# A hybrid attention and recurrence block: four whole input tiles added by VectorE, the second value quad ahead of the projection pairs, another last projection block

## The chip, the core and the metric

The kernel runs on one core of a Trainium2 chip. A core has five engines with a queue of instructions each: TensorE (PE, matmuls; its weight loads are listed as PEld), VectorE (DVE), ScalarE (ACT), GpSimd (POOL) and SyncE (SP, which here only issues transfers). Each engine works its own queue strictly in order; a wait on a semaphore holds everything behind it on that engine. The metric is device microseconds of one execution; less is better.

## The reference

```python
def hybrid_layer(x, layer, norm1_g, w_in, b_gate, lb_logits, hg_norm_g, w_o_sb, w_o_hg, w_out,
                 norm2_g, w_ff1, w_ff2):
    xn = rmsnorm(x, norm1_g[layer])
    u = xn @ w_in[layer].astype(f32)
    q_sb, k_sb, v_sb, f_raw, i_hg, q_hg, g_hg, gate_sb, gate_hg = jnp.split(u, list(c), axis=-1)
    o_sb = stick_breaking_attention(...)       # 8 heads of 64, causal, log space, blocks of 128 queries
    ...
    f = lb + (1.0 - lb) * sig                  # sig = sigmoid(f_raw)
    k_hg = (1.0 - lb) * jax.nn.sigmoid(-f_raw)
    o_hg = hgrn2_chunkwise(silu(q_hg), k_hg, i_hg, log(f))    # 4 heads of 128, chunks of 64
    o_hg = rmsnorm(o_hg, ...)
    o_hg = merge_heads(o_hg) * jax.nn.silu(g_hg)
    ...
```

1024 tokens of 1024 channels go through an RMSNorm; one wide projection gives queries, keys and values of 8 attention heads, the four inputs f, i, q, g of a 4-head gated recurrence (HGRN2), and two gates. Stick-breaking attention and the recurrence run on the same normalised input; their outputs are merged by sigmoid gates, projected, added to x, and followed by a squared-ReLU MLP of width 4096 and a last RMSNorm. All is float32.

## The kernel before

A float32 matrix is split into a high and a low part of a rounded format, hi = round(x) (a cast by ACT) and lo = x - hi (a subtraction by DVE), and a product is three matmuls: hi·hi, hi·lo and lo·hi. Names ending in h and l are such parts (xnh/xnl the normalised input, wv1h/wv1l the weights of the second value quad), names with r are raw weights as loaded.

The stages on PE are, in order:

- the front: transposes of x, the normalised input in eight tiles (half 0 and half 1 of the tokens, four each), the query/key projection of attention head 0 (`pjqk`), the value projection of heads 0 to 3 (`pjv` with wv0, 8 token blocks) and that of heads 4 to 7 (wv1, 8 token blocks, the job `j_v`). One token block is two steps of the stream `front`, 24 matmuls of 256 columns;
- four projection pairs (`ProjPair`): two blocks of 128 output columns are formed together from seven products m1 to m7 instead of eight, each of 12 matmuls of 512 columns (`ppX`, `ppY`, `ppZ`). This needs sums of input tiles: `early_whole` adds hi and lo back to whole tiles `xw`, `early_sums` adds whole tiles together and splits the sums into efh/efl. The eight blocks are the queries and keys of heads 1 to 7 and one further block, f of recurrence head 0;
- the attention loop over 64 items (8 heads, 8 query blocks): scores `z` from the tiles KS, QH, QL, a scan `rm` on DVE, a turn `pw` on PE, weights wTh/wTl, values `po`. KS, QH, QL of a head are written to DRAM by the projection and loaded again by SP (`qk_load`). Between items PE works off filler steps from the stream `st`: raw gate products (`raw_job`: `pga`, `pgq`, 36 matmuls of 512 columns), the i projection (`i_job`: `pji`), f, q and g projections (`hg_job`). `n_fill` filler jobs' steps are spread over the 64 items;
- the recurrence, head by head, with the rest of the stream as filler (`sl`, `pk` are its own products; `upto` bounds the filler for each head), then the merge, and the MLP.

What sets the order: each engine's queue is fixed when the program is built, from the order in which the code records operations and from buffer ownership. SP issues all loads one after another in the order of the code, and a load whose buffer is still in use holds those behind it. Raw weights have two buffers. POOL issues the stores of v, q and k, and in `early_whole(0)` it adds the four whole tiles of half 0.

Of the kernel before, what the change touches and what calls it, by code (L numbers as in the profile page):

```python
# [13 lines left out]
AF = mybir.ActivationFunctionType  # L14
ALU = mybir.AluOpType
# [24 lines left out]
def kernel(  # L40
# [67 lines left out]
    def after(ins, earlier):  # L108
        if earlier is not None and earlier.ins is not ins.ins:
            tc.add_manual_dep(ins.ins, earlier.ins.name, NOSYNC, reason="issue order")  # L110
        return ins
# [643 lines left out]
    def first_job():  # L755
        name, u_qk, ep = qk_item(0)
        u_qk.__class__ = FirstUnit
        u_v = v_unit(0)

        def body():  # L760
            v_ep = v_epilogue(0)
            for half, parts in enumerate((((0, 2), (2, 2)), ((0, 4),))):
                ps = bank(f"{name}_{half}")
                for b0, n in parts:
                    ts = slice(b0 * P, (b0 + n) * P)
                    yield from proj_half(ps[:, ts], u_qk.hl[0], xn.mov, KT, half, ts=ts)
                    if b0 + n == 4:
                        ep(ps, half)
                    if half == 0 and b0 > 0:
                        front.prefetch()  # L770
                    tb = 4 * half + b0
                    yield from token_steps("pjv0", u_v, xn, range(tb, tb + n), v_ep, tb == 0)

        return front.add([u_qk], body), u_qk, u_v
# [6 lines left out]
    def early_whole(half_, engine):  # L781
        for kp in range(KT // 2):
            h, l = (t.bitcast(F32) for t in xn.t[half_, kp])
            early[half_, kp // 2, kp % 2] = t = slot(f"xw{half_}{kp}")
            after(engine.tensor_tensor(out=t, in0=h, in1=l, op=ALU.add), last_power[0])

    early_forms = {}

# [130 lines left out]

    def qk_parts(h):  # L920
        return ((C_Q + h * DHS, DHS), (C_K + h * DHS, DHS)), qk_store(h)

    QB_ORDER = (7, 0, 6, 1, 5, 2, 4, 3)
    items = [(h, qb) for h in range(NHS) for qb in QB_ORDER]
# [167 lines left out]
    def i_job(h):  # L1092
        unit = wide_unit(f"wi{h}", W_IN, C_I + h * P)
        pair = {}

        def ep(ps, tb):
            i, c = tb // 2, tb % 2 * 256
            if c == 0:
                pair[i] = half(f"i{h}_{i}")
            nc.scalar.copy(pair[i][:, c : c + 256], ps)  # L1100
            if c:
                rows_ = irows[i * 256 : (i + 1) * 256, h * P : (h + 2) * P]
                nc.gpsimd.dma_start(
                    rows_.rearrange("(t p) c -> p t c", p=P),
                    pair.pop(i).rearrange("p (t c) -> p t c", t=2),
                )

        unit.late = h == 0

        def body():  # L1110
            for i, _ in enumerate(token_steps(f"pji{h}", unit, xn, range(NT), ep)):
                yield
                if unit.late and i == 6:
                    hi_behind[0] = turn_hi[0]
                    st.prefetch()
                    hi_behind[0] = None

        return st.add([unit], body)

    def i_load(h):  # L1120
        hg[h, "v"] = slot(f"v{h}")
# [467 lines left out]


    j_raw = [raw_job(0)]
    hg_job(0, "q")
    i_job(0)
    i_job(2)
    hg_job(0, "g")
    j_first_hg = j_hg[0]
    for h in range(1, NHG):
        hg_jobs(h)
        if h < NHG - 1:
            j_raw.append(raw_job(h))  # L1600
    j_raw += [raw_job(cb) for cb in range(len(j_raw), KT)]
    j_sb = [sb_job(cp) for cp in range(4)]

# [731 lines left out]
    lower_bounds()  # L2335
    front.advance(11, j_first)
    first_row()
    early_whole(0, nc.gpsimd)
    early_whole(1, nc.vector)
    early_sums()  # L2340
    blocks = [qk_parts(h) for h in range(1, NHS)] + [(((C_F, P),), f_epilogue(0))]
    proj = [ProjPair(i, *blocks[2 * i : 2 * i + 2]) for i in range(4)]
    front.finish(j_first)
    front.advance(8, j_v)
    proj[0].load()
    proj[0].split_plain()
    proj[0].m1()
# [1 line left out]
    for o, n in zip(proj, proj[1:] + [None]):  # L2349
        o.m2()  # L2350
        if n:
            n.load()
        o.m6()
        if not n:
            qk_load(0)
            v_load(0)
        o.m5()
        if n:
            n.split_plain()
        o.m7()  # L2360
        if n:
            n.m1()
            n.split_sums()
        o.m4()
        if not n:
            scores(*items[0])
            weights(*items[0])
        o.m3()
    v_split(0)
    front.advance(4, j_v)  # L2370
    scores(*items[1])
    front.advance(5, j_v)

    n_fill = 7 + 2 * 9 + 2 * 17
    n_first = 0
    ready = deque()
    wsums = out_weight_sums()
# [1 line left out]
    for i, it in enumerate(items):  # L2379
# [5 lines left out]
            next(wsums, None)  # L2385
        ahead = it[0] + 1
        if ahead < NHS and i % NHS in (2, 3, 5):
            if ahead == NHS // 2:
                front.finish(j_v)
            {2: qk_load, 3: v_load, 5: v_split}[i % NHS](ahead)  # L2390
        want = n_first + (i + 1) * (n_fill - n_first) // len(items)
        for _ in range(want - done):
            if front.pos < j_v:
                front.step()
            else:
                st.advance(1, j_first_hg)
        done = want
        before = ready.popleft() if ready else None

# [19 lines left out]
    for h in range(NHG + 1):  # L2419
# [2 lines left out]
        upto = (j_hg[2], j_hg[3], j_raw[6], j_sb[1], j_sb[3])[h]  # L2422
        if h > 0:
            i_load(h - 1)
        going = True
        while going:
            going = False
# [112 lines left out]
```

## Time and profile before

| | |
|---|---|
| median of 3 runs | 1492.26 us (1490.87 to 1496.12) |
| the profiled execution's own time | 1493.49 us |
| its span | 1491.8 us |
| PE busy | 1440.0 us, 97% of the span |
| DVE busy | 1106.6 us, 74% |
| ACT busy | 656.4 us, 44% |
| POOL busy | 177.2 us, 12% |
| mean granted PE clock | 0.985 |

The profiled execution lies 1.2 us above the median, and its span 1.7 us below its own time. A row of a timeline reads: start in us, duration in us, engine, line, operation, output<-inputs, shape, number of instructions run together, and in brackets how long the engine had been idle and what released it. A row of the table of waits reads: engine, line that waited, what it waited for, us in total, times, longest. A window row reads: stretch, length, busy us of PE, PEld, DVE, ACT and POOL with counts, granted PE clock, DMA share, GB/s.

### The profile page before, as it was taken

How to read it: one execution, taken by the hardware profiler on the slowest of the kernel's cores; microseconds unless marked ns; L12 is line 12 of the kernel's file. 1: busy time of each engine (PE TensorE's matmuls, PEld its weight loads, DVE VectorE, ACT ScalarE, POOL GpSimd, SP SyncE). 2: the span in 40 equal slices, each digit the busy share in tenths (PEclk: the TensorE clock that was granted, in tenths of full speed). 3: DMA queues.
4: the chain of work that ended last, by engine and by line, in shares of the span. 5: the costliest groups of instructions: out<-in, count | busy, mean ns of one | idle time of the engine just before them, and what ended most of it. 6: DMA issues, size and time to landing. Idle time of an engine off the chain costs nothing. (4 is left out here: it accounts for less than half of the span.)

```text
span 1491.8 us, 19878 instructions
## 1 busy us (share of the span) xinstructions
PE 1440.0 (97%) x7422; PEld 1223.7 (82%) x7422; DVE 1106.6 (74%) x1538; ACT 656.4 (44%) x1064; POOL 177.2 (12%) x322
## 2 busy tenths in 40 slices
PE   8899989899999999899998999999999999999997
PEld 8787879898888888788887888888888888888886
DVE  6964588788976789968775889766766656768755
ACT  6344456466232334343334485544444443433433
POOL 5212222232001012110011120000000000000031
PEclk9899999999999999999999999999999999999999
DMA  7146656765222258554559543444444985666824
GB/s 233 51 142 187 180 155 150 146 121 129 63 67 67 75 161 216 175 175 156 169 157 282 196 170 112 147 147 148 148 152 149 341 311 209 225 251 245 287 101 188
DMA packets 165945, 253.00 MB, mean 170 GB/s; under 512 B 27052, under 2 KB 95192, under 8 KB 165848
## 3 DMA queue, kind: packets, MB, share of 16 engines
q1 hardware_dynamic: 146392, 195.87, 40.1%
q0 software_dynamic: 15712, 49.30, 12.2%
q10 hardware_dynamic: 3744, 6.56, 1.2%
q8 instruction: 58, 0.95, 0.3%
q14 instruction: 39, 0.32, 0.1%
HBM read 181.43 MB, written 74.45 MB: 172 GB/s over the span
## 5 line engine op out<-in xcount | busy, mean ns | idle before, releaser
L972 DVE TENSOR_TENSOR_SCAN rm<-rm,bits 128x512 f32<-128x512 f32 (+6 forms) x72 | 87.6, 1223 | 20.2 <-ACT rm L946 19.8
L154 ACT CAST whid<-w 128x1024 fp32r<-128x1024 f32 x30 | 31.6, 1053 | 154.3 <-PE pm L131 90.1
L131 PE MATMUL pm<-wlod,sh 128*128 128x512 f32 x240 | 93.5, 389 | 0.1
L131 PE MATMUL pm<-whid,sl 128*128 128x512 f32 x240 | 93.4, 389 | 0.0
L131 PE MATMUL pm<-whid,sh 128*128 128x512 f32 x240 | 93.4, 389 | 0.0
L131 PE MATMUL pm<-tl,sh 128*128 128x512 f32 (+1 forms) x210 | 81.3, 387 | 0.0
L131 PE MATMUL pm<-th,sl 128*128 128x512 f32 (+1 forms) x210 | 81.3, 387 | 0.0
L131 PE MATMUL pm<-th,sh 128*128 128x512 f32 (+1 forms) x210 | 81.3, 387 | 0.0
L159 DVE TENSOR_TENSOR wlod<-w,whid 128x1024 fp32r<-128x1024 f32 x30 | 36.7, 1222 | 56.9 <-ACT whid L154 56.9
L2148 POOL TENSOR_SCALAR fss<-fss 128x1 f32<-128x1 f32 x8 | 4.0, 494 | 562.1 <-ACT fsc L2143 561.6
L159 DVE TENSOR_TENSOR sl<-sa,sh 128x1024 fp32r<-128x1024 f32 x56 | 68.2, 1218 | 0.5 <-ACT sh L154 0.5
L1020 ACT ACTIVATE wTh<-pw,minus_one 128x512 fp32r<-128x512 f32 (+2 forms) x96 | 53.4, 585 | 24.7 <-PE pw L134 23.9
L154 ACT CAST sh<-sa 128x1024 fp32r<-128x1024 f32 x56 | 57.2, 1046 | 6.7 <-DMA sa<-ad 6.7
L1026 DVE SCALAR_TENSOR_TENSOR wTl<-pw,wTh 128x512 fp32r<-128x512 f32 (+2 forms) x96 | 49.9, 545 | 7.5 <-ACT wTh L1020 6.9
L131 PEld LDWEIGHTS pm<-wlod,sh 128*128 128x128 f32 x240 | 45.0, 187 | 9.9 <-DVE wlod L159 0.6
L131 PEld LDWEIGHTS pm<-whid,sl 128*128 128x128 f32 x240 | 45.1, 188 | 9.4
L131 PEld LDWEIGHTS pm<-whid,sh 128*128 128x128 f32 x240 | 45.1, 188 | 9.3
L131 PE MATMUL pX<-sql,t1h 128*128 128x512 f32 x128 | 50.0, 391 | 0.1
L131 PE MATMUL pX<-sqh,t1l 128*128 128x512 f32 x128 | 49.8, 389 | 0.0
L131 PE MATMUL pX<-sqh,t1h 128*128 128x512 f32 x128 | 49.8, 389 | 0.0
L131 PE MATMUL po<-wTh,V 128*128 128x256 f32 x160 | 43.5, 303 | 3.7 <-ACT wTh L1020 3.7
L946 ACT ACTIVATE rm<-z 128x512 f32<-128x512 f32 (+3 forms) x96 | 44.0, 492 | 6.4 <-PE z L131 4.2
(965 smaller groups left out, 4610.0 us busy)
## 6 DMA issues: line engine op xcount, KB each, us to landing
w<-in_w_ff_dram SPq DMA_DIRECT2D x72, 512.0 KB, 5.1
sa<-ad SPq DMA_DIRECT2D x56, 512.0 KB, 6.4
ad<-a SPq DMA_DIRECT2D x32, 256.0 KB, 4.2
ad<-s SPq DMA_DIRECT2D x16, 512.0 KB, 5.7
tw<-in_w_out_dram POOLq DMA_DIRECT2D x24, 256.0 KB, 6.8
x<-in_x_dram SPq DMA_DIRECT2D x8, 512.0 KB, 8.6
qkh<-qkh POOLq DMA_DIRECT2D x16, 256.0 KB, 3.0
qkl<-qkl POOLq DMA_DIRECT2D x16, 256.0 KB, 3.2
```

Source lines behind the costliest of these rows:

```text
L131: return pe(nc.tensor.matmul(*a, **k))
L154: hi_last[0] = after(in_turn("act", nc.scalar.copy(dst, src)), hi_behind[0])
L159: nc.vector.tensor_tensor(out=dst, in0=src, in1=hi.bitcast(F32), op=ALU.subtract),
L946: nc.scalar.activation(rm[:, s0 : s0 + m], z[:, :m], AF.Sigmoid, scale=-0.125)
L972: sc = nc.vector.tensor_tensor_scan(out=rr, data0=rr, data1=bits[:, 1024 - nk + a : 1024 - nk + b][:, ::-1], initial=rm[:, b : b + 1] if i ...
L1020: nc.scalar.activation(th[:, 0:n, qs], src, AF.Identity, bias=minus_one),
L1026: nc.vector.scalar_tensor_tensor(out=tl[:, 0:n, qs], in0=src, scalar=-1.0, in1=th[:, 0:n, qs].bitcast(F32), op0=ALU.add, op1=ALU.subtract,),
L2148: nc.gpsimd.tensor_scalar(out=ssq, in0=ssq, scalar1=1.0 / D, scalar2=EPS, op0=ALU.mult, op1=ALU.add)
```

## The change

Six edits, all of order and place; the number of matmuls is the same.

1. The whole tiles of half 0 are added by VectorE instead of GpSimd, after those of half 1.
2. The loads and splits of the second value quad's weights (two casts, two subtractions) are recorded after the first job's second half instead of in the middle of it.
3. All 8 token blocks of the second value quad run before the pairs; before it was 4, and 4 behind the pairs.
4. The last block of the last pair is the g of recurrence head 0 instead of its f: its silu is stored to DRAM and loaded again by POOL when recurrence head 1 begins. The f of head 0 becomes a filler job.
5. `qk_load(0)` and `v_load(0)` come before m7 of the third pair instead of after m6 of the fourth, and the scores of the first two items between the fourth pair's products.
6. The filler stream is raw0, i0, raw1, i2, f0, q0, then heads 1 to 3 with raw2 between (before: raw0, q0, i0, i2, g0, then heads with raw1 to raw3 between). One raw job more lies in the attention loop (`n_fill` 59 to 66), and the loop no longer runs steps of the value quad. The special prefetch in `i_job` is gone.

```diff
--- before.py
+++ after.py
@@ -766,8 +766,6 @@
                     yield from proj_half(ps[:, ts], u_qk.hl[0], xn.mov, KT, half, ts=ts)
                     if b0 + n == 4:
                         ep(ps, half)
-                    if half == 0 and b0 > 0:
-                        front.prefetch()
                     tb = 4 * half + b0
                     yield from token_steps("pjv0", u_v, xn, range(tb, tb + n), v_ep, tb == 0)
 
@@ -782,7 +780,7 @@
         for kp in range(KT // 2):
             h, l = (t.bitcast(F32) for t in xn.t[half_, kp])
             early[half_, kp // 2, kp % 2] = t = slot(f"xw{half_}{kp}")
-            after(engine.tensor_tensor(out=t, in0=h, in1=l, op=ALU.add), last_power[0])
+            engine.tensor_tensor(out=t, in0=h, in1=l, op=ALU.add)
 
     early_forms = {}
 
@@ -919,6 +917,15 @@
 
     def qk_parts(h):
         return ((C_Q + h * DHS, DHS), (C_K + h * DHS, DHS)), qk_store(h)
+
+    gsd = dram("gs0", [P, T])
+
+    def g_store(src, half_):
+        cs = slice(half_ * 512, (half_ + 1) * 512)
+        t = half(f"g0_{half_}")
+        nc.scalar.activation(t, src, AF.Sigmoid)
+        mul(t, src, t)
+        nc.gpsimd.dma_start(gsd[:, cs], t)
 
     QB_ORDER = (7, 0, 6, 1, 5, 2, 4, 3)
     items = [(h, qb) for h in range(NHS) for qb in QB_ORDER]
@@ -1105,17 +1112,7 @@
                     pair.pop(i).rearrange("p (t c) -> p t c", t=2),
                 )
 
-        unit.late = h == 0
-
-        def body():
-            for i, _ in enumerate(token_steps(f"pji{h}", unit, xn, range(NT), ep)):
-                yield
-                if unit.late and i == 6:
-                    hi_behind[0] = turn_hi[0]
-                    st.prefetch()
-                    hi_behind[0] = None
-
-        return st.add([unit], body)
+        return st.add([unit], lambda: token_steps(f"pji{h}", unit, xn, range(NT), ep))
 
     def i_load(h):
         hg[h, "v"] = slot(f"v{h}")
@@ -1589,15 +1586,16 @@
 
 
     j_raw = [raw_job(0)]
+    i_job(0)
+    j_raw.append(raw_job(1))
+    i_job(2)
+    hg_job(0, "f")
     hg_job(0, "q")
-    i_job(0)
-    i_job(2)
-    hg_job(0, "g")
     j_first_hg = j_hg[0]
-    for h in range(1, NHG):
+    hg_jobs(1)
+    j_raw.append(raw_job(2))
+    for h in range(2, NHG):
         hg_jobs(h)
-        if h < NHG - 1:
-            j_raw.append(raw_job(h))
     j_raw += [raw_job(cb) for cb in range(len(j_raw), KT)]
     j_sb = [sb_job(cp) for cp in range(4)]
 
@@ -2335,13 +2333,14 @@
     lower_bounds()
     front.advance(11, j_first)
     first_row()
-    early_whole(0, nc.gpsimd)
+    front.prefetch()
     early_whole(1, nc.vector)
+    early_whole(0, nc.vector)
     early_sums()
-    blocks = [qk_parts(h) for h in range(1, NHS)] + [(((C_F, P),), f_epilogue(0))]
+    blocks = [qk_parts(h) for h in range(1, NHS)] + [(((C_GH, P),), g_store)]
     proj = [ProjPair(i, *blocks[2 * i : 2 * i + 2]) for i in range(4)]
     front.finish(j_first)
-    front.advance(8, j_v)
+    front.finish(j_v)
     proj[0].load()
     proj[0].split_plain()
     proj[0].m1()
@@ -2350,28 +2349,28 @@
         o.m2()
         if n:
             n.load()
+        else:
+            scores(*items[0])
         o.m6()
         if not n:
-            qk_load(0)
-            v_load(0)
+            weights(*items[0])
         o.m5()
         if n:
             n.split_plain()
+        else:
+            scores(*items[1])
+        if o is proj[-2]:
+            qk_load(0)
+            v_load(0)
         o.m7()
         if n:
             n.m1()
             n.split_sums()
         o.m4()
-        if not n:
-            scores(*items[0])
-            weights(*items[0])
         o.m3()
     v_split(0)
-    front.advance(4, j_v)
-    scores(*items[1])
-    front.advance(5, j_v)
-
-    n_fill = 7 + 2 * 9 + 2 * 17
+
+    n_fill = 2 * 7 + 2 * 9 + 2 * 17
     n_first = 0
     ready = deque()
     wsums = out_weight_sums()
@@ -2385,15 +2384,10 @@
             next(wsums, None)
         ahead = it[0] + 1
         if ahead < NHS and i % NHS in (2, 3, 5):
-            if ahead == NHS // 2:
-                front.finish(j_v)
             {2: qk_load, 3: v_load, 5: v_split}[i % NHS](ahead)
         want = n_first + (i + 1) * (n_fill - n_first) // len(items)
         for _ in range(want - done):
-            if front.pos < j_v:
-                front.step()
-            else:
-                st.advance(1, j_first_hg)
+            st.advance(1, j_first_hg)
         done = want
         before = ready.popleft() if ready else None
 
@@ -2422,6 +2416,9 @@
         upto = (j_hg[2], j_hg[3], j_raw[6], j_sb[1], j_sb[3])[h]
         if h > 0:
             i_load(h - 1)
+        if h == 1:
+            hg[0, "g"] = slot("g0")
+            nc.gpsimd.dma_start(hg[0, "g"], gsd)
         going = True
         while going:
             going = False
```

On DVE, near the end of the front (qkl is the low part of head 0's queries and keys, xnt a transpose of x in PSUM). Before:

```order
L159 TENSOR_TENSOR qkl_0_476<-pjqk_0_282,qkh_0_475 128x512
L159 TENSOR_TENSOR wv1l_486<-wv1r_481,wv1h_485 128x1024
L159 TENSOR_TENSOR wv1l_490<-wv1r_483,wv1h_489 128x1024
L335 SCALAR_TENSOR_TENSOR xnl_548<-xnt_0_549,prm,xnh_547 128x512
L335 SCALAR_TENSOR_TENSOR xnl_548<-xnt_0_556,prm,xnh_547 128x512
L335 SCALAR_TENSOR_TENSOR xnl_564<-xnt_0_565,prm,xnh_563 128x512
```

Now (the eight xnl of the second half follow the first qkl directly; this piece stands behind them):

```order
L159 TENSOR_TENSOR qkl_1_637<-pjqk_1_611,qkh_1_636 128x512
L159 TENSOR_TENSOR wv1l_744<-wv1r_739,wv1h_743 128x1024
L159 TENSOR_TENSOR wv1l_748<-wv1r_741,wv1h_747 128x1024
L783 TENSOR_TENSOR xw_751<-xnh_536,xnl_537 128x1024
L783 TENSOR_TENSOR xw_753<-xnh_552,xnl_553 128x1024
L783 TENSOR_TENSOR xw_755<-xnh_568,xnl_569 128x1024
L783 TENSOR_TENSOR xw_757<-xnh_584,xnl_585 128x1024
L783 TENSOR_TENSOR xw_759<-xnh_247,xnl_248 128x1024
```

The two wv1l subtractions moved from ahead of the eight xnl to behind the second qkl, and DVE has eight whole-tile additions there, four of them POOL's before.

On SP, the loads at the start of the attention loop (KS and QH of the next head, wi0r/wi2r the raw i weights, wga1r the raw gate weights, wq0r those of q). Before:

```order
L139 DMA QL_1732<-qkl_102 64x1024 x2
L139 DMA wq0r_1776<-in_w_in_dram 128x8x128
L139 DMA wi0r_1782<-in_w_in_dram 128x4x256
L139 DMA wi0r_1784<-in_w_in_dram 128x4x256
L139 DMA wi2r_1967<-in_w_in_dram 128x4x256
L139 DMA wi2r_1969<-in_w_in_dram 128x4x256
L139 DMA KS_2041<-qkh_103 64x1024
```

Now:

```order
L139 DMA QL_1737<-qkl_102 64x1024 x2
L139 DMA wi0r_1750<-in_w_in_dram 128x4x256
L139 DMA wi0r_1752<-in_w_in_dram 128x4x256
L139 DMA wga1r_1762<-in_w_in_dram 128x8x128
L139 DMA wga1r_1764<-in_w_in_dram 128x8x128
L139 DMA wi2r_1940<-in_w_in_dram 128x4x256
L139 DMA wi2r_1942<-in_w_in_dram 128x4x256
L139 DMA KS_2074<-qkh_103 64x1024
```

The load of wq0r is gone from here and the two of wga1r stand between those of wi0r and wi2r.

On PE, the end of the recurrence's levels of head 3 (sl the level products, pk the state's, pot and pys filler). Before:

```order
L131 MATMUL pys_1_6122<-asbh_5660,wo01l_5900 128x512
L131 MATMUL sl_5_6133<-q_5176,k_5065 32x32 x16
L131 MATMUL pys_1_6122<-asbh_5757,wo01h_5899 128x512
L131 MATMUL pys_1_6122<-asbl_5758,wo01h_5899 128x512
L131 MATMUL pys_1_6122<-asbh_5757,wo01l_5900 128x512
L131 MATMUL pys_1_6122<-asbh_5869,wo01h_5899 128x512
L131 MATMUL pys_1_6122<-asbl_5870,wo01h_5899 128x512
L131 MATMUL pys_1_6122<-asbh_5869,wo01l_5900 128x512
L131 MATMUL sl_6_6169<-q_5176,k_5065 64x64 x8
L134 MATMUL pk_0_6193<-ident,k_5065 128x128 x4
```

Now:

```order
L131 MATMUL pys_1_6104<-asbh_5824,wo01l_5845 128x512
L131 MATMUL sl_4_0_6126<-q_5138,k_5024 128x128 x4
L131 MATMUL sl_4_1_6131<-q_5138,k_5024 128x128 x4
L134 MATMUL pot_1_6144<-ident,hon_1_6007 128x128 x4
L131 MATMUL sl_5_6150<-q_5138,k_5024 32x32 x16
L131 MATMUL sl_6_6175<-q_5138,k_5024 64x64 x8
L134 MATMUL pk_0_6199<-ident,k_5024 128x128 x4
```

Between sl_4 and pk there stood 36 filler matmuls of 512 columns (the last 12 around sl_5 are seen above); now there is none beside the transposes pot. From the end of head 2's pk to head 3's, the filler has 126 such matmuls, where it had 162.

## The prediction

> **What bounds the kernel now.** I read the page first, then PE's table of waits, then the windows, and only then single rows around each wait.
>
> ```profile
> PE 1440.0 (97%) x7422; PEld 1223.7 (82%) x7422; DVE 1106.6 (74%) x1538; ACT 656.4 (44%) x1064; POOL 177.2 (12%) x322
> PE ppar L215 <- DVE xnl L335: 9.0, 1, 9.0
> PE z L131 <- DMA QH<-qkh: 8.0, 2, 4.4
> PE pwW L131 <- DVE h L1395: 4.2, 1, 4.2
> PE sl L131 <- DVE pp L167: 4.0, 1, 4.0
> PE po L131 <- ACT wTh L1020: 3.7, 3, 1.9
> PE pw L134 <- ACT i L1100: 3.5, 1, 3.5
> PE pgq L131 <- ACT wga0t L154: 2.5, 1, 2.5
> PE pk L134 <- DVE k L167: 1.4, 1, 1.4
> ```
>
> PE is busy 97% and the change leaves its matmuls alone, so what can move is PE's idle time, some 50 us, and the slow clock behind each wait. The change touches all but pwW of these. The windows say where they lie, and that the clock falls with them (column behind POOL):
>
> ```profile
> 40.00:60.00 20.00, 15.91 (x93) 14.28 (x94) 19.48 (x27) 1.84 (x5) 4.29 (x5) 0.79 0.20 57
> 60.00:80.00 20.00, 20.00 (x149) 19.12 (x149) 18.99 (x20) 13.03 (x18) 2.72 (x4) 1.00 0.15 50
> 140.00:160.00 20.00, 16.39 (x75) 13.45 (x74) 6.76 (x10) 6.85 (x11) 3.47 (x5) 0.91 0.91 226
> 160.00:180.00 20.00, 17.49 (x122) 16.07 (x122) 12.25 (x16) 8.87 (x20) 6.61 (x16) 0.96 0.71 192
> 200.00:220.00 20.00, 15.60 (x85) 13.28 (x84) 14.60 (x22) 8.80 (x19) 4.66 (x13) 0.91 0.85 211
> 260.00:280.00 20.00, 15.06 (x98) 14.20 (x98) 13.85 (x18) 9.39 (x21) 4.55 (x12) 0.84 0.48 90
> 600.00:650.00 50.00, 44.59 (x262) 37.57 (x261) 45.27 (x76) 21.55 (x42) 7.18 (x11) 0.93 0.54 172
> ```
>
> **The front (edits 1 to 3).** The 9.0 us are the largest term. The timeline of DVE, POOL and PE shows their cause:
>
> ```profile
> 14.23 2.36 DVE L159 TENSOR_TENSOR wv0l<-wv0r,wv0h 128x1024 fp32r<-128x1024 f32 x2
> 30.98 12.05 DVE L159 TENSOR_TENSOR wv1l<-wv1r,wv1h 128x1024 fp32r<-128x1024 f32 x2
> 32.70 9.25 POOL L785 TENSOR_TENSOR xw<-xnh,xnl 128x1024 f32<-128x1024 f32 x4
> 42.96 3.37 DVE L335 SCALAR_TENSOR_TENSOR xnl<-xnt,prm,xnh 128x512 fp32r<-128x512 f32 x5
> 43.75 0.32 PE L215 MATMUL ppar<-ident,prow 36*128 36x36 f32 x1 [9.01 <-DVE xnl L335]
> 50.99 0.39 PE L131 MATMUL pjqk<-xnh,wqk0wlo 128*128 128x512 f32 x1
> 51.67 0.39 PE L131 MATMUL pjqk<-xnh,wqk0wlo 128*128 128x512 f32 x1
> 51.90 0.28 PE L131 MATMUL pjv<-wv0h,xnh 128*128 128x256 f32 x1
> ```
>
> Two subtractions that take 2.36 us for wv0 took 12.05 for wv1, and the 9.7 us more are POOL's 9.25 of additions: the two engines did not work side by side. DVE's xnl stood behind, and PE behind them. In the changed order the eight xnl follow the first qkl at once, and POOL adds nothing. With 3.37/5 = 0.67 us each from about 32.4 on, they end at 37.7, a pair each 1.35 us; PE comes to ppar at 43.75 − 9.01 = 34.74 and uses a pair per 6 matmuls at 0.227 us (51.67 − 50.99 over three), 1.36 us, so it finds each there. `pjqk` then ends at 34.74 + 0.3 + 24×0.227 = 40.5 where it ended at 51.9: **−11.4 us**, 9.0 of the wait and the rest slow clock (0.79 in that window).
>
> This time must not be lost again ahead of the pairs, since DVE was full there (19.48 and 18.99 of 20). It gets 4 more whole tiles and the wv1 subtractions:
>
> ```profile
> L785 POOL TENSOR_TENSOR xw<-xnh,xnl x4: 2329/2335/2372, 32.7 to 39.6; 128x1024 f32<-128x1024 f32 x4
> L785 DVE TENSOR_TENSOR xw<-xnh,xnl x4: 1214/1216/1220, 49.7 to 54.6; 128x1024 f32<-128x1024 f32 x4
> 54.97 0.37 ACT L663 COPY v<-pjv 128x256 f32<-128x256 f32 x1 [2.29 <-PE pjv L131]
> 57.85 0.37 ACT L663 COPY v<-pjv 128x256 f32<-128x256 f32 x1 [2.51 <-PE pjv L131]
> 77.79 1.22 DVE L159 TENSOR_TENSOR wlob<-wp0b,whib 128x1024 fp32r<-128x1024 f32 x1 [0.39 <-ACT whib L154]
> 80.40 0.39 PE L131 MATMUL ppX<-efh,whib 128*128 128x512 f32 x1
> ```
>
> A token block of the value quad takes PE 57.85 − 54.97 = 2.88 us; 4 of them now run ahead of the pairs, 11.5 us, so m1 begins when it did (40.5 + 4×2.88 + 8×2.88 = 75.1, and m6 at 80.5 against 80.40), with 11.5 us of later work done. DVE is free at 42, does wv1 to 44.4 (first needed by the second quad at 52.0), then eight whole tiles. The first sum of whole tiles starts at 44.4 + 8×1.14 = 53.5, where it started at 55.7 (54.6 + 1.14); the rest of the chain is the same, so wlob is ready by 77, some 3 us ahead of m6. Hence nothing for the moved additions; their cover is that second quad. Without it they would cost 4×1.14 + 2.36 = 6.9 less these 3.
>
> **The end of the pairs (edits 4, 5).** PE's first wait for QH:
>
> ```profile
> 138.84 0.45 SPq L139 DMA_DIRECT2D QH<-qkh  x1
> 149.45 0.73 PE L131 MATMUL z<-KS,QH 128*128 128x512 f32 x2 [3.61 <-DMA QH<-qkh]
> 150.97 0.63 PE L131 MATMUL ppX<-xnl,w54h 128*128 128x512 f32 x1
> 151.40 0.63 PE L131 MATMUL ppX<-xnh,w54l 128*128 128x512 f32 x1
> 202.48 0.65 SPq L139 DMA_DIRECT2D QH<-qkh  x1
> 216.36 1.19 PE L131 MATMUL z<-KS,QH 128*128 128x512 f32 x2 [4.40 <-DMA QH<-qkh]
> QH<-qkh SPq DMA_DIRECT2D x2, 256.0 KB, 12.4
> wi2r<-in_w_in_dram SPq DMA_DIRECT2D x2, 512.0 KB, 5.4
> ```
>
> QH was issued at 138.84, when the fourth pair's m6 let go of its buffer, and its data came 10.6 us later. Its issue now stands a pair earlier on SP, and the buffers it takes are let go by the first two pairs: that is 20 us and more ahead of z. The 3.61 us go, and with them 9 matmuls at 0.427 in place of 0.227 us (151.40 − 150.97; they are 0.63 long where 0.39 is usual): 3.61 + 1.8 = **−5.4 us**. g's silu store is two halves of ACT, DVE and POOL work in place of f's; none of these engines is full in 140 to 160 (6.76, 6.85 and 3.47 of 20), so nothing.
>
> On the slow clock the Trainium skill ("TensorE: Matmul & The Clock Gate", "What's actually happening") says that PE falls to half rate after an idle window of about 3.4 us. The rows agree for the waits of 3.6 and 4.4, but the wait of 2.5 for pgq is also followed by a clock of 0.96. By the rule each long wait adds up to 1.7 us; the sum would differ by under 1.
>
> **The start of the attention loop (edit 6).** The second wait for QH, 4.40 at 216.36, has its load issued at 202.48, behind wi2r on SP, with 12.4 us to landing since the DMA engines were at 0.85. PE had 216.36 − 4.40 − 202.48 = 9.5 us of work in that time. Now SP comes to it when wga1's splits let a buffer go, and by the filler that stands from there to the second head's z PE has 14 to 15. The price with the slow rows behind is 4.4 + 1.4 = 5.8; I take **−4.5** (0 to −5.8).
>
> The third, 3.5 for pw, and 1.42 behind it for po:
>
> ```profile
> 270.79 1.04 ACT L154 CAST wg0h<-wg0r 128x1024 fp32r<-128x1024 f32 x1 [6.78 <-DMA wg0r<-in_w_in_dram]
> ```
>
> ACT stood 6.78 us at this cast while its copy of i and its wTh were queued behind. wg0 leaves the loop; wf0 takes its place behind wi2's buffer, its cast some 6 us after its issue, nearly the landing time (5.4 for wi2r). Of 3.5 + 1.4 + 1.4 = 6.3 I take **−4** (0 to −6.3).
>
> New there are the loads of wi0 and wga1 close ahead of their casts, each behind a buffer that the one before must let go. ACT or DVE can stand at these as ACT stood for wg0: **+1.5** (0, as behind the pair's weights, to 4, two thirds of that case). q0 now is the last filler before the recurrence needs q: **+0.5** (0 to 1.5, below pk's 1.4). The wait for wga0t, 2.5, has the same cast ahead of it as before; I leave it.
>
> **The recurrence (edit 6).** The raw job that went into the attention loop is missing here. In head 3's stretch PE waited 4.0 + 1.4 = 5.4 us for DVE, which was at 45.27 of 50. Between the second head's pk and the third's the filler falls from 162 to 126 matmuls, 36×0.227 = 8.2 us of PE; DVE loses the job's splits:
>
> ```profile
> 400.97 1.22 DVE L1395 TENSOR_TENSOR wga1r<-wga1r,wga1r 128x1024 f32<-128x1024 f32 x1
> ```
>
> Two of this size and three of half of it (two more for the weights, and the sum of p1 and p4), at 1.22 and some 0.69, are 4.5 us. Where DVE sets the pace, PE gains no time from less filler beyond these 4.5: idle grows by 8.2 − 4.5 = 3.7. I take **+4** (1.5, with 2.4 us of DVE's waits for loads gone, to 7, with DVE's part not shortened in the stretch that counts). In the attention loop the same 8.2 us fill nothing that the trace shows as idle; it counts once, as PE work.
>
> **Sum.** −11.4 −5.4 −4.5 −4 +1.5 +0.5 +4 = −19.3, from the profiled execution's 1493.5: **1474 us**, or 1473 as the median stands 1.2 lower. With all ends good it is −28 (1465), with all bad −11.4 −5.4 +4 +1.5 +7 = −4.3 (1489).
>
> **The rivals.**
>
> A: *the attention loop only trades its waits.* SP's order there is new, every raw weight has just two buffers, and a wait removed in a chain of loads may stand a load further on. Then the second and third wait bring nothing, and with +1.5, +0.5 and the recurrence's full 7 it is 1493.5 − 16.8 + 9 = **1486**. For it: three waits in 176 to 273 had three different loads as cause. Against: PE has more filler per item.
>
> B, on the other side: *casts at the head of ACT's queue.* wi0, wga1, wi2, wf0 come in a row, each cast waiting 6.78 as wg0h did, PE losing 6.3 each. Without the gain on the second and third wait, and with the recurrence's 4 and q0's 0.5, −12.3 is there to be eaten; from two such waits it is even, and from three (+18.9) it is slower: **1500**. Against: the row of wg0h is the only cast in the loop that stood so long.
>
> C: *the change doesn't do what it says in the front.* If the 12.05 us are not POOL's doing (the trace shows only that they coincide) but a late input of the second subtraction, the wait goes with wv1 to another place, behind the second qkl, and stops the second quad: −11.4 becomes −1.7, which gives **1484**.
>
> D: *DVE becomes the bound ahead of the pairs.* Should its chain slip by the 6.9 us added, wlob is there at 79.0 + 6.9 = 85.9, for m6's third matmul at 80.9: +5.0, **1479**. The Trainium skill speaks for it ("Perfetto Trace Analysis", "Optimizing Scalar/DVE Operations"): a saturated DVE is to hand work to others; it adds that a hand-over to GpSimd may not help, as they share a port. POOL's 2.33 us for DVE's 1.22, and DVE standing for all of them, agree with the second half.
>
> **How the numbers follow.** Forecast 0.58, A 0.20, B 0.07, C 0.08, D 0.07. The range 1463 to 1489 holds the forecast's own ends, A, C and D at their times, and leaves out B and the bad ends of A. A measurement of this kernel tells 0.3%, 4.5 us, from no change: below 1487.8 is faster. Of the forecast's 0.58 nearly all is, of A 0.13, of C 0.06, of D all: 0.83; no change 0.10; slower 0.07 from B.
>
> **What would show it.** In the changed profile PE should have no wait over 1 us at ppar, POOL no xw row, DVE's wv1l 2.4 us; the window 40 to 60 PE full at clock 1.00; m6 at about 80 and the fourth pair ahead of the loop ending near where it did; no wait for QH at the first z and one under 2 us at the second head's; PE's waits for DVE in the recurrence 8 to 11 us in place of 5.4. A wait of several us at m1, m6 or pjv's second quad proves C or D; rows of casts idle over 5 us for wi or wga loads prove B. The forecast is wrong if PE's idle time in 40 to 300 does not fall by some 15 us, or if the recurrence's grows by over 8.

## The result, and the profile after

| | before | changed |
|---|---|---|
| median | 1492.64 us (1490.87 to 1496.12, 4 runs) | 1474.63 us (1470.48 to 1475.80, 4 runs) |
| profiled execution | 1493.49 us, span 1491.8 | 1475.80 us, span 1474.1 |
| mean granted PE clock | 0.985 | 0.988 |

The ratio is 0.9872, 95% interval 0.9845 to 0.9898: 1.3% faster, where 1474 was forecast.

From PE's table of waits in the changed kernel (engine, line, what it waited for, us in total, times, longest):

```profile
PE sl L131 <- DVE pp L167: 5.7, 2, 4.2
PE pwW L131 <- DVE h L1392: 5.5, 1, 5.5
PE po L131 <- DVE wTl L1033: 4.2, 4, 2.3
PE pji L131 <- DVE wTl L1033: 2.4, 1, 2.4
PE po L131 <- ACT wTh L1027: 2.0, 3, 1.1
PE pjqk L131 <- DVE xnl L335: 1.8, 1, 1.8
PE pgq L131 <- ACT wga0t L154: 1.4, 1, 1.4
PE pgq L131 <- DVE wga0t L159: 1.1, 1, 1.1
PE pw L134 <- ACT rm L953: 1.1, 1, 1.1
```

The 9.0 at ppar and both waits for QH are gone; the 1.8 at pjqk lie in the first half of the front, at 11.92, ahead of what the edits move. What remains from the fourth pair to the end of the attention loop is short, and spread over po, pji, pgq and pw. Three waits are longer than before: the one for pp in the recurrence (5.7, where it was 4.0 and 1.4 more at pk), the one for h in the merge, and po's for wTl (4.2, 2.7 before). Windows of 20 us of the changed kernel (columns as before):

```profile
40.00:60.00 20.00, 20.00 (x160) 19.61 (x160) 17.81 (x21) 5.03 (x10) 3.62 (x6) 1.00 0.43 106
140.00:160.00 20.00, 19.83 (x95) 16.20 (x93) 14.55 (x20) 11.02 (x20) 6.83 (x17) 1.00 0.87 256
160.00:180.00 20.00, 17.50 (x100) 15.21 (x101) 13.93 (x18) 12.32 (x23) 4.62 (x12) 0.91 0.70 215
180.00:200.00 20.00, 17.74 (x131) 17.17 (x130) 17.28 (x25) 10.24 (x24) 4.48 (x10) 0.91 0.66 173
260.00:280.00 20.00, 15.66 (x122) 14.72 (x122) 15.95 (x21) 10.77 (x25) 4.88 (x8) 1.00 0.78 185
```

40 to 60 is full at clock 1.00 (15.91 and 0.79 before) and 140 to 160 nearly so. The stretches 160 to 200 and 260 to 280 still have 2 to 4 us of idle PE each, the first two with a lowered clock.

To place the gain, I took for each kernel the start of certain matmuls minus the streaming time of all matmuls ahead of them in PE's order (0.2265 us per 512 columns, at least 0.05 for one). The difference is the time lost up to there, with a constant part that is equal in all kernels, so that only the differences down a column mean something; the table has its growth by stage, in us. "To pair 1" ends at m1's first matmul, "pairs" at the last `ppX`, "to po" at the first values, "loop" at the last values, "recurrence" at head 3's pk, "rest" at the last matmul of the MLP.

| kernel | to pair 1 | pairs | to po | loop | recurrence | rest | all |
|---|---|---|---|---|---|---|---|
| before | 26.9 | 5.4 | 6.0 | 43.7 | 43.3 | 19.3 | 144.6 |
| changed | 17.7 | 0.3 | 5.7 | 38.4 | 43.9 | 21.0 | 127.0 |
| changed, profiled again | 15.9 | 0.3 | 5.7 | 41.3 | 43.7 | 19.4 | 126.3 |
| GpSimd adds beside xnl | 15.7 | 1.1 | 4.0 | 41.6 | 43.8 | 19.5 | 125.7 |
| before, edit 1 only | 17.5 | 8.8 | 7.6 | 44.6 | 44.1 | 18.3 | 140.9 |
| before, edits 1 and 2 | 15.4 | 12.6 | 7.1 | 46.0 | 43.7 | 20.6 | 145.4 |
| before, edits 1 to 3 | 16.3 | 0.2 | 12.6 | 45.5 | 43.0 | 20.0 | 137.6 |
| changed without edit 5 | 16.0 | 0.2 | 9.0 | 38.6 | 43.8 | 18.2 | 125.8 |
| second raw job back | 16.0 | 0.4 | 4.9 | 31.9 | 43.7 | 19.5 | 116.4 |
| old stream order | 16.0 | 0.4 | 4.6 | 33.6 | 45.0 | 19.5 | 119.1 |
| old order, old prefetch | 16.4 | 0.3 | 4.0 | 32.9 | 44.0 | 20.2 | 117.8 |

So the changed kernel won 9 to 11 us before the pairs, 5 in the pairs, 2 to 5 in the loop, and lost nothing in the recurrence. One execution differs from another by 1 to 3 us in a stage: in its first profile the changed kernel came to the first `pjv` at 16.13 us, in its second at 14.38, and the kernel before at 14.66.

### The profile page after: what moved, and what is told of

It reads as the page before. It is cut to its first block, busy times and chain, and to the rows that moved or that the text cites. A ratio compares the mean times of both kernels' runs of the same rounds, so it can differ in the third digit from the quotient of the medians.

```text
span 1474.1 us, 19891 instructions
## 1 busy us (share of the span) xinstructions
PE 1437.2 (97%) x7422; PEld 1222.6 (83%) x7422; DVE 1102.5 (75%) x1542; ACT 656.5 (45%) x1064; POOL 173.8 (12%) x321
## 5 line engine op out<-in xcount | busy, mean ns | idle before, releaser
L131 PE MATMUL po<-wTl,V 128*128 128x256 f32 x160 | 42.1, 296 | 4.3 <-DVE wTl L1033 4.2
L131 PEld LDWEIGHTS pm<-tl,sh 128*128 128x128 f32 x210 | 39.4, 188 | 8.2
```

The source lines that it names most:

```text
L131: return pe(nc.tensor.matmul(*a, **k))
```

## The experiments

All are timed against the kernel before on the same chip; where no interval is named, medians are meant. The kernel before spread more on these chips (1477.8 to 1495.6) than on the first, so the intervals of the ratios are some 0.3 to 0.7% to each side, and small differences are read from the stages above. Three chips were used: one for the first four experiments, one for "Edit 5 undone", the second raw job, the old order and the filler in head 3's levels, one for the rest. Where kernels of different chips are set side by side, that is a comparison of medians alone.

**What held up the second half's input.** GpSimd adds the four whole tiles again, beside the xnl; the rest is the changed kernel.

```diff
-            engine.tensor_tensor(out=t, in0=h, in1=l, op=ALU.add)
+            r = engine.tensor_tensor(out=t, in0=h, in1=l, op=ALU.add)
+            if half_ == 0:
+                after(r, last_power[0])
...
+    early_whole(0, nc.gpsimd)
     front.advance(11, j_first)
...
     early_whole(1, nc.vector)
-    early_whole(0, nc.vector)
```

> The changed kernel, with the four whole tiles of half 0 added by GpSimd again, recorded ahead of the first job's second half so that they run beside the eight xnl. If GpSimd's additions hold up whatever DVE does (the prediction's reading), the eight xnl, 5.4 us in the changed kernel, last about 14 to 15, PE waits some 8 to 9 us ahead of or in pjqk, and the time rises by 7 to 11 us, less up to 4.6 us for four additions fewer on DVE if these are on its path. If they hold up only an operation that takes both inputs from SBUF (xnl takes one from PSUM), xnl keeps 5.4 us and the time is the changed kernel's within 2 us. If GpSimd was not the cause, wv1l takes 2.4 us here too and nothing else moves.

1474.4 us, beside 1474.6 and 1474.0 for the changed kernel: no difference. The timeline of DVE and POOL in this kernel:

```profile
32.10 5.36 DVE L335 SCALAR_TENSOR_TENSOR xnl<-xnt,prm,xnh 128x512 fp32r<-128x512 f32 x8 [1.41 <-ACT xnh L332]
32.35 9.45 POOL L783 TENSOR_TENSOR xw<-xnh,xnl 128x1024 f32<-128x1024 f32 x4
37.60 4.23 DVE L226 TENSOR_TENSOR lmx<-prm 128x4 f32<-128x4 f32 x1
41.86 0.24 DVE L230 TENSOR_TENSOR le<-prm,lmx 128x4 f32<-128x4 f32 x2
```

The eight xnl, whose xnt lies in PSUM, take 5.36 us with GpSimd adding beside them, exactly as without. The operation behind them, on 4 columns and with both its inputs in SBUF, takes 4.23 us, until GpSimd's last addition ends at 41.80; operations of that size take some 0.2 elsewhere. The copy of prm just before it, out of PSUM, takes 0.18. So GpSimd did hold DVE up, but only operations with both inputs in SBUF: in the kernel before, the wv1 subtractions. Moving these two behind the xnl (edit 2) is enough; who adds the whole tiles (edit 1) makes no difference to the time of the changed kernel. The Trainium skill ("SBUF — State Buffer", "SBUF: two separate sides") says the same, that GpSimd and a DVE operation with two SBUF inputs lock each other out for the length of an instruction. Here the wait was longer than that: GpSimd's instructions end about every 2.36 us (9.45/4), and the small operation waited from 37.60 past an end at about 39.4 to the last one.

**Edit 1 alone**, in the kernel before.

```diff
-            after(engine.tensor_tensor(out=t, in0=h, in1=l, op=ALU.add), last_power[0])
+            engine.tensor_tensor(out=t, in0=h, in1=l, op=ALU.add)
...
-    early_whole(0, nc.gpsimd)
     early_whole(1, nc.vector)
+    early_whole(0, nc.vector)
```

> The kernel before, with only the four whole tiles of half 0 moved to DVE; the two wv1 subtractions stay ahead of the xnl, half of the second quad stays behind the pairs. If GpSimd held up DVE: wv1l takes 2.4 us in place of 12, PE's wait at ppar falls from 9.0 to under 1.5 us, and PE then stands ahead of m6 instead, since DVE's chain to wlob ends only some 3 us sooner: the time falls by 2 to 5 us. Rival, a late input of the second subtraction: wv1l stays at about 12 us and the time at 1492, within 2.

1491.05 us, ratio 1.0006 (0.9971 to 1.0041). Its timeline:

```profile
30.91 2.35 DVE L159 TENSOR_TENSOR wv1l<-wv1r,wv1h 128x1024 fp32r<-128x1024 f32 x2
75.52 0.79 PE L131 MATMUL ppX<-efh,whib 128*128 128x512 f32 x1 [3.36 <-ACT whib L154]
```

wv1l is 2.35 us, so the late-input rival falls. Of the 9.4 us won up to the first pair (26.9 to 17.5) the pairs lose 3.4, where PE waits for the weights' sums, and the way to the first values, the loop and the recurrence 1.6, 0.9 and 0.8. Some 4 are left in this execution (1489.7); the medians show none of it, where a fall of 2 to 5 us was expected.

**Edits 1 and 2 without the cover**: four token blocks of the second quad stay behind the pairs.

```diff
-                    if half == 0 and b0 > 0:
-                        front.prefetch()
...
-            after(engine.tensor_tensor(out=t, in0=h, in1=l, op=ALU.add), last_power[0])
+            engine.tensor_tensor(out=t, in0=h, in1=l, op=ALU.add)
...
-    early_whole(0, nc.gpsimd)
+    front.prefetch()
     early_whole(1, nc.vector)
+    early_whole(0, nc.vector)
```

> The kernel before with edits 1 and 2 only: whole tiles by DVE, the wv1 split behind the second qkl, but four token blocks of the second quad still behind the pairs. If those four blocks are the cover of DVE's chain (the prediction), PE comes to m1 and m6 about 11.5 us sooner than DVE is ready, wlob is there at about 79 as in the changed kernel, PE waits 6 to 10 us between the value quad and m6, and the time is 1487 to 1492. If DVE has slack without it, PE does not wait there and the time is 1480 to 1484.

1492.4 us, ratio 1.0016 (0.9981 to 1.0050). PE's waits in this kernel:

```profile
PE z L131 <- DMA QH<-qkh: 6.8, 2, 5.0
PE ppX L131 <- DVE wloa L159: 2.9, 1, 2.9
PE ppX L131 <- ACT whib L154: 2.9, 1, 2.9
```

The front is the best of all (15.4), 11.5 us won. The pairs give back 7.2 of them (12.6 against 5.4), with 6.5 us of PE's waits for the weights' sums (0.7 for wlob beside the two rows): DVE's chain is not ready without those four blocks. The way to the first values, the loop and the rest lose 1.1, 2.3 and 1.3 more than before, and in all nothing is left (145.4 against 144.6). With edit 3 added, in the next experiment, the median is 6.8 us lower on the same chip and the two kernels' times do not overlap: edit 3 is what makes edits 1 and 2 worth anything.

**Edits 1 to 3 alone**, the attention loop as it was. To the edit of the experiment before it adds:

```diff
...
-    front.advance(8, j_v)
+    front.finish(j_v)
...
-    front.advance(4, j_v)
     scores(*items[1])
-    front.advance(5, j_v)
```

> The kernel before with edits 1 to 3 only: the pairs, the attention loop and the recurrence are left as they were. The prediction's front term alone, -11.4: 1481. By the two traces, in which the changed kernel is 9.1 us ahead when the first pair starts: 1483 to 1484. If the later waits grow with an earlier start (QH's loads come no sooner), 1486 to 1490: the waits for QH then exceed 3.6 and 4.4 us.

1485.6 us (1482.6 to 1489.3), ratio 0.9970 (0.9932 to 1.0007), not clear of no change. It lies between what the two traces gave, 1483 to 1484, and the case of longer waits, 1486 to 1490, and its second head's wait for QH, 4.6, is only a little longer than 4.4. SP's row for head 0's QH, and PE's waits:

```profile
118.37 0.60 SPq L139 DMA_DIRECT2D QH<-qkh  x1
PE z L131 <- DMA QH<-qkh: 4.6, 1, 4.6
PE ppY L131 <- DVE pv L880: 3.6, 1, 3.6
PE pw L134 <- ACT i L1098: 3.3, 1, 3.3
```

QH of head 0 goes out at 118.37 where it went out at 138.84, though its call stands where it did. Without edit 3, in the experiment before, it went out at 137.80, so edit 3 does it. The likely reason is that the finished second quad has let its tiles go: these tiles and QH come from one pool in the code, and KS, issued just ahead of QH, waited 19.7 us for a tile in the kernel before and none here. Which tile it takes was not traced. The pairs lose 0.2. But the loss is back behind them (12.6 to the first values, 6.0 before), the 3.6 for pv among it, and the loop waits as before.

**Edit 5 undone** in the changed kernel: loads and scores of the first items at their old places.

```diff
-        else:
-            scores(*items[0])
         o.m6()
         if not n:
-            weights(*items[0])
+            qk_load(0)
+            v_load(0)
...
-        else:
-            scores(*items[1])
-        if o is proj[-2]:
-            qk_load(0)
-            v_load(0)
...
         o.m4()
+        if not n:
+            scores(*items[0])
+            weights(*items[0])
         o.m3()
     v_split(0)
+    scores(*items[1])
```

> The changed kernel with edit 5 undone: KS, QH, QL and the values of head 0 are loaded behind m6 of the fourth pair again, and the scores of the first two items stand where they stood. The prediction's term: the wait ahead of the fourth pair's last products is back, +5.4 with its slow matmuls, 1479 to 1480. Rival, from the run with the front's edits alone (no wait for QH there, but 3.6 us at m3 for a subtraction of DVE): the loads come in time by edit 4's free buffers or by the order alone, PE waits 3 to 4 us at m3 or the first turn instead, same size but another cause. If neither, the time stays within 2 us.

1475.2 us, no difference from the changed kernel. The wait for QH does not return: QH goes out at 118.01 here and at 119.93 in the changed kernel, so its issue does not hang on edit 5. The way to the first values is 3.3 us longer (9.0 against 5.7); the total does not show it, the merge's wait for h being 3.2 here and 5.5 there. What edit 5 is worth lies inside that spread.

**The second raw gate job back in the recurrence.**

```diff
     i_job(0)
-    j_raw.append(raw_job(1))
     i_job(2)
...
-    hg_jobs(1)
-    j_raw.append(raw_job(2))
-    for h in range(2, NHG):
+    for h in range(1, NHG):
         hg_jobs(h)
+        if h < NHG - 1:
+            j_raw.append(raw_job(h))
...
-    n_fill = 2 * 7 + 2 * 9 + 2 * 17
+    n_fill = 7 + 2 * 9 + 2 * 17
```

> The changed kernel with the second raw gate job back in the recurrence (36 matmuls of 512 columns and its splits), everything else of the stream as changed. The prediction has the recurrence lose 4 us by that move: the recurrence's waits are then 5.4 or less, and pk of head 2 to pk of head 3 is 60 to 61 us in place of 52.6 for 8.2 us more of filler; the time falls by up to 4 if the attention loop does as well with less filler. Rival, from the two traces (the stretch is shorter by the whole 8.2 us, the waits differ by 0.3): the move cost the recurrence nothing, and the time is the changed kernel's or above it by what the attention loop loses, 0 to +5.

1465.2 us (1464.7 to 1465.9), ratio 0.9835 (0.9801 to 0.9869): 9 us faster than the changed kernel, where one expectation had up to 4 and the other none. It was measured on the same chip as the changed kernel without edit 5 (1475.2) and with more filler (1474.0), and its slowest run (1465.9) lies 5 us below the fastest of theirs (1471.0). The recurrence loses 43.7, against 43.9 and 43.7, and from head 2's pk to head 3's takes 60.5 us again (533.4 to 593.9). The windows of that stretch in the kernel before and then in the changed one tell why the move was free there:

```profile
561.38:622.24 60.86, 55.34 (x328) 46.47 (x327) 55.84 (x95) 25.31 (x47) 13.00 (x17) 0.97 0.73 203
```

```profile
550.33:602.94 52.61, 46.88 (x292) 40.88 (x291) 50.85 (x90) 21.84 (x41) 11.49 (x16) 0.94 0.71 188
```

The stretch is 8.25 us shorter. DVE's work fell by 5.0 (55.84 to 50.85), and its idle time from 5.0 to 1.8, which is the rest. The loop, in contrast, loses 31.9 in place of 38.4 and 41.3. Two rows of the changed kernel name waits that came with the job:

```profile
180.69 1.23 DVE L1392 TENSOR_TENSOR wga1r<-wga1r,wga1r 128x1024 f32<-128x1024 f32 x1 [1.67 <-DMA wga1r<-in_w_in_dram]
266.07 1.05 ACT L154 CAST wq0h<-wq0r 128x1024 fp32r<-128x1024 f32 x1 [3.86 <-DMA wq0r<-in_w_in_dram]
```

DVE stands for wga1's load with three wTl queued behind, and PE waits 2.26 us at po; ACT stands for wq0's, which follows the job's loads on SP, and PE waits 1.06 and 2.39. These are 5.7 us. With the job back in the recurrence these waits are not there:

```profile
PE po L131 <- DVE wTl L1033: 4.5, 8, 0.9
PE pgq L131 <- ACT wga0t L154: 2.5, 1, 2.5
PE po L131 <- ACT wTh L1027: 1.2, 3, 0.5
PE pw L134 <- DVE rm L979: 1.2, 1, 1.2
```

Between the first values (164.6) and the last no wait is longer than 1.2 us; the 2.5 at pgq come ahead of them, at 161.8. The run moves the job as a whole: what its loads cost, and what its work on ACT and DVE, it does not tell apart.

**The stream's old order** under edits 1 to 5.

```diff
+    hg_job(0, "q")
     i_job(0)
-    j_raw.append(raw_job(1))
     i_job(2)
     hg_job(0, "f")
-    hg_job(0, "q")
... (the loop over heads and n_fill as in the experiment before)
```

> The changed kernel with the stream's old order (raw0, q0, i0, i2, then f0 where g0 stood, raw1 to raw3 between the heads) and 59 filler steps. By the prediction's terms (4.5 and 4 lost again, 1.5, 0.5 and 4 won): +2.5, 1477. By the two traces (attention loop 5.7 us ahead, recurrence about 1 behind): +4 to +5, 1479, with a wait of 4 to 5 us for QH at the second head and one of 3 us behind ACT's or DVE's wait for raw weights. If the waits only trade places: within 2 us.

1467.6 us (1465.5 to 1468.0), ratio 0.9848 (0.9813 to 0.9882): faster than the change by 7, where two of the three expectations had it slower by 2.5 to 5 and the third within 2. One row:

```profile
PE z L131 <- DMA QH<-qkh: 2.0, 1, 2.0
```

The second head's QH costs 2.0 us here, 4.4 in the kernel before, so more than half of that wait went without edit 6's order; and the 3.5 us at a turn behind ACT's cast are gone altogether.

**The old prefetch rule** of the first i job on top of it: the next weights are split behind the turn in progress.

```diff
-        return st.add([unit], lambda: token_steps(f"pji{h}", unit, xn, range(NT), ep))
+        unit.late = h == 0
+        def body():
...
+                if unit.late and i == 6:
+                    hi_behind[0] = turn_hi[0]
+                    st.prefetch()
+                    hi_behind[0] = None
+        return st.add([unit], body)
```

> The changed kernel with the stream's old order (as in the run before of that name) and also the old prefetch rule of the first i job: the next weights are split behind the turn in progress, at its seventh step. If that rule made ACT stand at a late cast ahead of its copy of i (3.5 us of PE at the turn, 1.4 behind it, 6.3 with the slow matmuls), that wait is back and the time goes from 1467.6 to 1471 to 1474. If the order of the loads or the f0 in g0's place took that wait away, the time stays at 1467 to 1469 and no turn waits for ACT's copy of i.

1467.1 us: that rule was not the cause. ACT's row shows that a long stand at a cast need not cost PE much:

```profile
246.63 1.05 ACT L154 CAST wf0h<-wf0r 128x1024 fp32r<-128x1024 f32 x1 [3.53 <-DMA wf0r<-in_w_in_dram]
```

ACT stood 3.53 us for wf0, and the longest wait of PE behind it was 1.4.

**Edit 4 undone**, with the second raw job back: f of head 0 in the pairs, g as filler, no store and reload.

```diff
-    blocks = [...] + [(((C_GH, P),), g_store)]
+    blocks = [...] + [(((C_F, P),), f_epilogue(0))]
...
-    hg_job(0, "f")
+    hg_job(0, "g")
...
-        if h == 1:
-            hg[0, "g"] = slot("g0")
-            nc.gpsimd.dma_start(hg[0, "g"], gsd)
```

> The kernel with the second raw gate job back in the recurrence (1465.2), with edit 4 undone: the last block of the fourth pair is f of head 0, g of head 0 is a filler job, nothing is stored to DRAM and loaded again. If edit 4 is only a swap of two blocks of the same size: 1465 within 2. If it is what took the wait for ACT's cast out of the loop (wg0 is gone there, wf0 stands in its place), a wait of 3 to 5 us at a turn returns and the time is 1469 to 1471.

1465.7 us, no difference: with this order edit 4 is a swap of two blocks.

**More filler in head 3's levels** of the changed kernel.

```diff
-        upto = (j_hg[2], j_hg[3], j_raw[6], j_sb[1], j_sb[3])[h]
+        upto = (j_hg[2], j_hg[3], j_raw[6], j_sb[2], j_sb[3])[h]
```

> The changed kernel with the filler bound of head 3's levels raised by one merge job group, so that 54 more filler matmuls stand between sl_4 and pk there. If DVE sets the end of that stretch and filler lies beside it, the waits of 4.2 and 1.5 us go and the time falls by 3 to 6 us, unless the stretch behind, which has that filler less, waits instead (then within 2 us). If filler brings DVE work of its own (each merge group has additions on DVE), sl_5 and sl_6 come later and less than half of the 5.7 us is won.

1474.0 us, no difference. The waits for pp go and others come:

```profile
PE pk L134 <- DVE k L167: 3.0, 2, 2.8
PE pot L134 <- DVE hon L167: 2.9, 1, 2.9
```

DVE sets the end of that stretch, and filler moves the place at which PE waits for it.

**The third part of the first raw weights split earlier**, in the kernel with the second raw job back.

```diff
+            if cb == 0:
+                u.split_t()
             yield from steps_of(ps, 0, 0, 0, 0, True)
...
-            if cb == 0:
-                u.split_t()
             st.prefetch()
```

> The kernel with the second raw gate job back in the recurrence (1465.2), with one edit more: the third part of the first raw gate weights (wga0t) is split before the job's first step, not behind its first half. PE's wait of 2.5 us for that cast then goes, with up to 1.4 of slow matmuls behind it: 1461 to 1464. If ACT or DVE only hand the delay to the turns beside it, 1465 within 1.

1466.7 us (1464.4 to 1470.4), not faster; it was expected at 1461 to 1464, or at 1465 if the delay is handed on. The wait of 2.5 at pgq is gone, and this stands in its place:

```profile
PE pw L134 <- DVE rm L979: 3.2, 1, 3.2
```

The way to the first values loses 1.0 in place of 4.9, and the loop 37.1 in place of 31.9: handed on.

**The changed kernel again**, on one chip with three of the kernels above: the old prefetch rule, the earlier split and edit 4 undone.

> The changed kernel itself beside the three others on one chip, for their comparison: 1474 within 3; the kernel with the second raw gate job in the recurrence measured 1465, 9 less, on another chip. If the two chips differ, the distance between this and the other three is not 9.

1474.0 us (1471.4 to 1475.2, 9 runs), and 1467.1, 1466.7 and 1465.7 for the three in that order. The distance, 7 to 8 us on this chip, is not the chip's.

## Why the prediction was right

The sum was right to within 2 us (1474 forecast; 1474.6 the median, 1475.8 the profiled execution), and not all of its terms were.

- **The front, −11.4: right in size, and in the mechanism as far as GpSimd goes.** The stage won 9.2 us in the first profile and 11.0 in the second; `pjqk` ended at 42.1 and at 40.2, where 40.5 was forecast. wv1l took 2.35 us, the xnl 5.36 without a gap, and PE found them in time:

```profile
34.10 5.36 DVE L335 SCALAR_TENSOR_TENSOR xnl<-xnt,prm,xnh 128x512 fp32r<-128x512 f32 x8 [1.62 <-ACT xnh L332]
36.33 0.25 PE L215 MATMUL ppar<-ident,prow 36*128 36x36 f32 x1
43.50 2.35 DVE L159 TENSOR_TENSOR wv1l<-wv1r,wv1h 128x1024 fp32r<-128x1024 f32 x2
78.19 1.23 DVE L159 TENSOR_TENSOR wlob<-wp0b,whib 128x1024 fp32r<-128x1024 f32 x1 [0.56 <-ACT whib L154]
82.10 0.39 PE L131 MATMUL ppX<-efh,whib 128*128 128x512 f32 x1
```

  wlob is ready at 79.4, 3.1 us ahead of its first use at 82.55 (m6's third matmul); the prediction had some 3. What it did not see is that GpSimd held up the two wv1 subtractions and not DVE as a whole: once edit 2 has moved these, GpSimd's additions do no harm beside the xnl, and edit 1 is not needed.
- **The moved additions at nothing, covered by the second quad: right.** Without the cover nothing was gained (1492.4). The price named for that case, 6.9 less 3, was too low: PE waits 6.5 us there and the pairs lose 7.2 more.
- **The end of the pairs, −5.4: right in size, wrong in the edit.** The step that failed is that edit 5 brings QH's load forward, past a buffer that the fourth pair holds; edit 3 does (118.37 with edits 1 to 3 alone, 118.01 without edit 5). But the wait is not the whole of it: the pairs and the way to the first values together lose 11.4 before, 12.8 with edits 1 to 3, 9.2 without edit 5 and 6.0 in the changed kernel, so the gain stays only with the edits behind edit 3. Edit 5's part, 3.2 to 3.3 us there, does not show in the total.
- **The second head's QH, −4.5: right that it goes** (no wait for QH is left), but with the old order it fell to 2.0 as well.
- **The third wait, −4: too much for the changed kernel.** The wait for wg0's cast is gone, but wf0's cast stood 2.72 us and wq0's 3.86, and behind wq0's PE waited 1.06 and 2.39, 3.45 of the 4.93. With the second raw job back wq0's cast does not stand, so these 3.45 are part of what the next term left out.
- **The new loads, +1.5 (0 to 4): far too little.** This is the term that was most mis-sized. The raw job with its loads costs the loop 6.5 (38.4 against 31.9), in the second profile 9.4. It is rival B's mechanism, work queued behind a split on DVE and ACT that waits for its load, at a third to a half of its 18.9. The waits named above come to 5.7 of it.
- **The recurrence, +4: wrong.** The step that failed is that PE's idle time there grows by 8.2 − 4.5: DVE's own idle time fell by 3.2 us as well, and the stage lost 43.3 before and 43.9 and 43.7 after. The term's lower end, 1.5, had 2.4 us of this in it; the measured 0.4 to 0.6 lies below it.

By stage, the front and the pairs were forecast at −16.8 and came at −14.3 and −16.1, the loop at −6.5 and came at −5.3 and −2.4, the recurrence at +4 and came at +0.6 and +0.4. What the loop and the front fell short by, 3.7 and 4.8 us, the recurrence did not take, 3.4 and 3.6: two errors cancelled, and that the sum came so close is luck. From the table's first two rows −9.2, −5.1, −0.3, −5.3, +0.6 and +1.7 make −17.6, where the two profiled executions differ by 17.7. With all ends good the terms add up to −27.4, 1466, not −28 and 1465.

Two of the prediction's own signs failed. It called itself wrong if PE's idle time between 40 and 300 us did not fall by some 15: it fell by 10.8 in the first profile (238.7 busy of 260 before, 249.5 after) and by 9.9 in the second. The window was badly cut, since 5.3 of the 9.0 us at ppar lie ahead of 40; from 30 to 300 the fall is 16.0 and 15.2. And PE's waits for DVE in the recurrence were to be 8 to 11 us; they are 5.7, which is the recurrence's term failing. The other signs came: no wait at ppar, no xw row of POOL, a full window from 40 to 60 at clock 1.00, m6 at 82.1 and 80.3, no wait for QH.

Not settled: why the loop loses only 33 to 34 us with the old order under edits 1 to 5, and 45.5 under edits 1 to 3. The prefetch rule is not it; edit 4 made no difference with another order, edit 5 none with a third. Which of the two does it with the old order was not run.

## What to carry to other kernels

Moving filler out of a stage whose pace another engine sets cost that stage nothing here, since the filler had brought 5.0 us of work and 3.2 us of waiting to that engine; what such a move costs must be looked for where the filler is put, in the loads that come with it and in what is queued behind their first use on ACT and DVE. When a wait is won early in a pipeline, ask what work fills the time up to the next engine that is not ready: without it the gain is gone at the next stage, as it was twice here. Of the versions measured the lowest median takes edits 1 to 5 and the new order without the second raw job: 1465.2 us, 0.9835 of the kernel before (0.9801 to 0.9869). Undoing edit 4 in it leaves it where it is (1465.7).

## What the runs showed of the hardware

- GpSimd's additions held up a DVE operation with two inputs in SBUF, even one of 4 columns (4.23 us), over more than one GpSimd instruction (2.36 us each), and left operations with one input in PSUM alone (5.36 us for eight, with and without).
- Two DVE subtractions with two SBUF inputs each took 12.05 us, where 2.35 is their time in the kernel in which GpSimd adds nothing beside them. The first took its usual 1.22. The second, begun at 32.12, just ahead of GpSimd's four additions (32.70 to 41.95), took 10.92 and ended 1.1 us after the last of them.
